# Wider warming matmuls ahead of the memory keys, and three more behind the first six products

## The chip, the cores and the metric

The kernel runs on one core of a Trainium2 chip. The metric is the device time of one execution in microseconds (us), median of several runs; lower is better.

## The reference

One layer of a hybrid decoder trunk in float32: a prompt of 1024 tokens and 8 sample tokens share the weights. Cut to what matters here:

```python
z = x @ w_in                                  # one projection, split among the branches and gates
mkv = (mem_prompt @ w_mem_kv).reshape(1, 256, 2, 4, 256)
mk, mv = mkv[:, :, 0], mkv[:, :, 1]           # memory keys and values, for 256 memory tokens
a_out = rg_lru(causal_conv(xr)) * gelu(yr)
s_out = sliding_window_attention(q, k, v, sinks)
c_out = mem_attn(xq, mk, mv)                  # cross-attention into the memory
merged = sum(gates[n] * (br @ w_branch[n]) for n, br in enumerate((a_out, s_out, c_out)))
h = layer_norm(ALPHA * x + merged @ w_out)
y = layer_norm(ALPHA * h + (silu(h @ w_gate) * (h @ w_up)) @ w_down)
```

`mk` and `mv` are also outputs. `mem_prompt` has 256 rows of 1024, `w_mem_kv` 1024 x 2048.

## The kernel before

The kernel is written with a scheduler that follows the order of the code within the stage at issue (the orders of SP, ACT, DVE and PE are kept as written). Transposed tiles hold features on the 128 partitions and tokens along the free axis. A float32 product is made of three: each operand is cut into a high part (rounded to the multiplier's format, by ACT) and a low part (the rest, by DVE), and `mm3` (lines 128 to 130) issues high x high, high x low and low x high into one PSUM sum. `split` (lines 82 and 83) is that cut: ACT writes the `..h` tile, DVE the `..l` tile.

The program begins with `mem_kv`, which computes the memory keys and values. Its pieces:

- `mem_raw(k)` loads two of the eight feature tiles of the memory, `mem_split(k)` cuts them into `memh`, `meml`; all eight stay as `memx[0]` to `memx[7]`.
- `fetch(n)` loads one half (512 columns) of a weight tile `wm`, n = 0 to 31, five steps ahead; `cut(n)` cuts it into `wm_h` and `wm_l`, three steps ahead. The first half, `wm0`, and the first memory tiles are loaded and cut in two pieces.
- `key(n)` for n = 0 to 15 issues 12 products of 256 columns, four terms of three; two steps make one bank `mk`. `value(n)` for n = 16 to 31 issues 12 products into two banks `mv`. `put` copies a finished bank with ACT and stores it with a DMA from POOL.
- Within the same loop, `x_quarter` loads the input in eight pieces of 516 KB, and `moving` (the generator `combos`) makes sums of them on DVE and cuts them into `th` and `tl` for the projection that follows (`fast_step`, whose products write `ub`, `uc`, `ud`).

The tiles for `wm_h` go round in five buffers and those for `wm_l` in four, so a cut waits until PE has used the tile four or five steps back. The loads go out on SP's queue (two of the first on ACT's), in the order of the code, each into a buffer that a cut has set free.

Ahead of all products stand the warming matmuls (line 503): `WARM` = 20 products of the constant tile `ones` with itself, 128 columns each, into a bank `warm` that nobody reads. They wait only for the memset of `ones`.

Of the kernel before, what the change touches and what calls it, by code (L numbers as in the profile page):

```python
# [18 lines left out]
P = 128  # L19
# [7 lines left out]
NM = 256  # L27
# [6 lines left out]
BANKS = {"mm": 3, "s": 2, "t": 2, "o": 1}  # L34
HT = T // 2
FIRST = 6
WARM = 20
ORDERED = {mybir.EngineType.SP, mybir.EngineType.Activation, mybir.EngineType.DVE, mybir.EngineType.PE}
QN = T // 4
QS = 264  # L40
# [18 lines left out]
class Builder:  # L59
# [380 lines left out]
    def mem_kv(self, moving, xs, load, quarters):  # L440


        nc, io = self.nc, self.io
        h = D // 2
        memx, raws, pairs, sums = [], {}, {}, {}
        order = [(f, p) for f in ((0, 0), (0, 1), (1, 1), (1, 0)) for p in range(2)]

        def put(bank, name, m):
            raw = self.ph.tile([P, 256], F32, tag="kvraw", name=f"{name}r{m}", bufs=4)
            nc.scalar.copy(raw, bank[1][:, :256])  # L450
            self.idle.append(bank[0])
            nc.gpsimd.dma_start(self.scr[name][:, m, :], raw)

        def mem_raw(k, queue=None, pieces=1):
            src = io["memT"][:, 2 * k * NM:(2 * k + 2) * NM]
            raws["mem", k] = self.half_raw(src, 2 * NM, f"mem{k}", k < 3, queue, pieces)

        def mem_split(k, between=()):
            raw = raws.pop(("mem", k))
            for i in range(2):  # L460
                for f in between[:i]:
                    f()
                memx.append(tuple(self.ph.tile([P, NM], F32R, tag="mem", name=f"mem{e}{2 * k + i}", bufs=16)
                                  for e in "hl"))
                self.split(*memx[-1], raw[:, i * NM:(i + 1) * NM])

        def fetch(n, queue=None, pieces=1):
            if n < 16:
                src = io["wmk"][n // 2][:, n % 2 * h:(n % 2 + 1) * h]
            else:  # L470
                src = io["wmv"][(n - 16) // 2][:, n % 2 * h:(n % 2 + 1) * h]
            raws[n] = self.half_raw(src, h, f"wm{n}r", 4 < n < 28 and n % 3 == 0, queue, pieces)

        def cut(n, pieces=1):
            pairs[n] = self.half_pair(f"wm{n}_")
            raw = raws.pop(n)
            for i in range(pieces):
                cols = slice(i * h // pieces, (i + 1) * h // pieces)
                self.split(*(t[:, cols] for t in (*pairs[n], raw)))
                if i + 1 < pieces:  # L480
                    yield

        def key(n):
            m, e = n // 2, n % 2
            if e == 0:
                sums[m] = self.take(f"mk{m}")
            hi, lo = pairs.pop(n)
            cols = [slice(i * P, (i + 1) * P) for i in range(4)]
            self.mm3(sums[m][1][:, :NM], [((hi[:, w], lo[:, w]), memx[4 * e + i]) for i, w in enumerate(cols)], e == 1, e == 0)

        def value(n):
            g, j = (n - 16) // 4, n % 4
            if j == 0:
                sums[g] = [self.take(f"mv{g}_{tt}") for tt in range(2)]
            hi, lo = pairs.pop(n)
            cols = [slice(i * 256, (i + 1) * 256) for i in range(2)]
            for tt in range(2):
                xs_ = [tuple(a[:, tt * P:(tt + 1) * P] for a in memx[2 * j + i]) for i in range(2)]
                self.mm3(sums[g][tt][1][:, :256], [(x, (hi[:, w], lo[:, w])) for x, w in zip(xs_, cols)], j == 3, j == 0)

        warm = self.bank("o", "warm")
        for _ in range(WARM):
            nc.tensor.matmul(warm[:, :P], self.ones, self.ones, start=True, stop=True)
        other = nc.scalar
        for f in (partial(mem_raw, 0, pieces=2), partial(fetch, 0, other, 2), partial(mem_raw, 1, other), partial(fetch, 1),
                  partial(mem_raw, 2), partial(mem_raw, 3), partial(fetch, 2), partial(fetch, 3), partial(fetch, 4)):
            f()
        first, rest = cut(0, 2), lambda n: deque(cut(n), 0)
        mem_split(0, (partial(next, first),))
        deque(first, 0)  # L510
        for f in (partial(mem_split, 1), partial(rest, 1), partial(mem_split, 2), partial(mem_split, 3), partial(rest, 2)):
            f()
        due = -3.5
        for n in range(32):
            if n + 5 < 32:
                fetch(n + 5)
            elif n == 28:
                load()
            if n % 2 == 0 and n < 16:
                (f, th), p = order[n // 2]  # L520
                xs[(f, th), p] = self.x_quarter(f, th, p)
            if n + 3 < 32:
                rest(n + 3)
            elif n > 29:
                quarters[n - 30]()
            due += 0.6
            if due > 0:
                due -= next(moving)
            (key if n < 16 else value)(n)
            if 0 < n <= 16 and n % 2 == 0:  # L530
                put(sums.pop(n // 2 - 1), "mk", n // 2 - 1)
            if n > 16 and n % 4 == 0:
                g = (n - 16) // 4 - 1
                for tt, ps in enumerate(sums.pop(g)):
                    put(ps, "mv", 2 * g + tt)
        for tt, ps in enumerate(sums.pop(3)):
            put(ps, "mv", 6 + tt)
# [1322 lines left out]
```

## Time and profile before

| | |
|---|---|
| time, median of 3 runs | 1896.47 us (1895.70 to 1896.66) |
| span of the profiled execution, first to last instruction | 1894.5 us |
| time around the span, against the median | 1.97 us |
| PE busy (matmuls) | 1880.9 us, 99% of the span |
| DVE / ACT busy | 1398.8 us (74%) / 1056.6 us (56%) |
| DMA | 302.18 MB, 160 GB/s on average |
| waits of PE up to 120 us | 1.1 (start), 0.9 (`memh`), 0.3 (`u2s`) |

The profile gives one execution. A row of the timeline has the start and the duration in us, the engine, the line, the operation, the tiles (buffer numbers left out), the shape, and in square brackets the idle time of that engine ahead of it and what ended it. Matmuls are pipelined: the duration of one holds its way through the array, so the time that it costs is read from start to start. A row of a table by stretches has the stretch, its length, the busy time of PE, PE's weight loads, DVE, ACT and POOL with the number of instructions, then the granted clock of TensorE, the share of the DMA engines in use and GB/s. A value such as 1.04 for that share counts as full.

### The profile page before, as it was taken

What the parts mean: (1) busy time and instruction counts of PE and PEld (TensorE: products, weight loads), DVE (VectorE), ACT (ScalarE), POOL (GpSimd) and SP (SyncE); (2) the same over time, 40 slices, a digit from 0 to 9 for tenths busy, and PEclk for the clock granted to TensorE, in tenths of its full rate; (3) what the DMA queues carried; (4) which work ended last, traced back from release to release, by engine and by line L of the source; (5) the groups of instructions that cost most, each with busy time, mean ns of one, the idle gap of its engine ahead of it and who ended that gap; (6) DMA issues with size and microseconds to landing.
All of it is one profiled execution on the core that took longest, in us unless ns stands there. A gap on an engine that the chain in (4) does not pass through costs nothing.

```text
span 1894.5 us, 38166 instructions
## 1 busy us (share of the span) xinstructions
PE 1880.9 (99%) x14836; PEld 1865.1 (98%) x14836; DVE 1398.8 (74%) x2736; ACT 1056.6 (56%) x2199; POOL 126.7 (7%) x190
## 2 busy tenths in 40 slices
PE   9999999999999999999999999999999999999998
PEld 9999999999999999999999999999999999999998
DVE  7878878888788757579787567776667667858486
ACT  6575676666676656578774234543433433636454
POOL 1000012110000000022210000000000000001200
PEclk9999999999999999999999999999999999999999
DMA  9535345446444377546525251233355235758872
GB/s 333 171 109 171 114 142 172 137 143 221 143 159 152 108 239 253 190 144 198 155 79 188 90 190 57 68 112 115 112 165 199 99 123 185 263 131 271 173 216 90
DMA packets 176261, 302.18 MB, mean 160 GB/s; under 512 B 18944, under 2 KB 93136, under 8 KB 176080
## 3 DMA queue, kind: packets, MB, share of 16 engines
q1 hardware_dynamic: 168976, 280.12, 45.0%
q0 software_dynamic: 4224, 14.78, 4.0%
q10 hardware_dynamic: 2880, 4.85, 0.7%
q8 instruction: 116, 1.90, 0.4%
q14 instruction: 65, 0.53, 0.1%
HBM read 217.97 MB, written 85.89 MB: 160 GB/s over the span
## 4 chain that ended last, share of the span: by engine, by line
PE 92%; DVE 3%; DMA 2%; ACT 1%; issue 1%; SPq 0%; ACTq 0%; DVEq 0%
PE ub L271 5%; PE ub L273 5%; PE ub L272 5%; PE ubfg L272 4%; PE ubfg L273 4%; PE ubfg L271 4%; PE ud L273 3%; PE ud L272 3%; PE ud L271 3%; PE udfg L271 2%; PE udfg L272 2%; PE udfg L273 2%; PE ubf L271 2%; PE op L128 2%; PE ubf L272 2%; PE ubf L273 2%
## 5 line engine op out<-in xcount | busy, mean ns | idle before, releaser
L712 ACT ACTIVATE bp<-bp,bst 128x257 f32<-128x257 f32 (+1 forms) x128 | 62.9, 493 | 37.3 <-DVE bst L706 37.2
L271 PE MATMUL ub<-th,u_6h 128*128 128x258 f32 x240 | 68.8, 287 | 1.9 <-DVE zb L312 1.8
L706 DVE CUSTOM_DVE_ANT_0 bp<-bs,mask,nsnk 128x256 f32<-128x256 f32 (+1 forms) x128 | 55.8, 462 | 19.0 <-PE bs L703 18.6
L271 PE MATMUL ub<-th,u_4h 128*128 128x258 f32 x240 | 68.2, 284 | 0.3 <-ACT u2s L305 0.3
L273 PE MATMUL ud<-th,u_5l 128*128 128x258 f32 x240 | 68.2, 284 | 0.0
L271 PE MATMUL ud<-th,u_5h 128*128 128x258 f32 x240 | 68.1, 284 | 0.0
L271 PE MATMUL ub<-th,u_0h 128*128 128x258 f32 x240 | 68.1, 284 | 0.0
L273 PE MATMUL ud<-th,u_1l 128*128 128x258 f32 x240 | 68.1, 284 | 0.0
L271 PE MATMUL ub<-th,u_2h 128*128 128x258 f32 x240 | 68.1, 284 | 0.0
L273 PE MATMUL ub<-th,u_4l 128*128 128x258 f32 x240 | 68.0, 284 | 0.0
L271 PE MATMUL ud<-th,u_1h 128*128 128x258 f32 x240 | 68.0, 284 | 0.0
L273 PE MATMUL ub<-th,u_2l 128*128 128x258 f32 x240 | 68.0, 284 | 0.0
L273 PE MATMUL uc<-th,u_3l 128*128 128x258 f32 x240 | 68.0, 283 | 0.0
L271 PE MATMUL uc<-th,u_3h 128*128 128x258 f32 x240 | 68.0, 283 | 0.0
L273 PE MATMUL ub<-th,u_0l 128*128 128x258 f32 x240 | 68.0, 283 | 0.0
L273 PE MATMUL ub<-th,u_6l 128*128 128x258 f32 x240 | 68.0, 283 | 0.0
L272 PE MATMUL ud<-tl,u_5h 128*128 128x258 f32 x240 | 67.7, 282 | 0.0
L272 PE MATMUL ub<-tl,u_0h 128*128 128x258 f32 x240 | 67.6, 282 | 0.0
L272 PE MATMUL ub<-tl,u_6h 128*128 128x258 f32 x240 | 67.6, 282 | 0.0
L272 PE MATMUL ub<-tl,u_4h 128*128 128x258 f32 x240 | 67.6, 282 | 0.0
L272 PE MATMUL ud<-tl,u_1h 128*128 128x258 f32 x240 | 67.6, 282 | 0.0
L272 PE MATMUL uc<-tl,u_3h 128*128 128x258 f32 x240 | 67.6, 282 | 0.0
(959 smaller groups left out, 8257.6 us busy)
## 6 DMA issues: line engine op xcount, KB each, us to landing
ur<-win SPq DMA_DIRECT2D x120, 256.0 KB, 3.0
urfg<-wgu SPq DMA_DIRECT2D x80, 256.0 KB, 2.7
scr_f<-G SPq DMA_DIRECT2D x22, 516.0 KB, 2.9
f<-scr_f SPq DMA_DIRECT2D x16, 516.0 KB, 4.0
fs<-scr_t SPq DMA_DIRECT2D x16, 516.0 KB, 7.2
dck<-cmk SPq DMA_DIRECT2D x32, 256.0 KB, 4.4
dcv<-cmvT SPq DMA_DIRECT2D x32, 256.0 KB, 4.6
urf<-wdn SPq DMA_DIRECT2D x32, 256.0 KB, 3.4
```

The lines of the kernel that those rows point to most:

```text
L128: nc.tensor.matmul(ps, sh, mh, start=opens and i == 0, stop=False)
L271: mm(sh[:, w], xh, start=opens and k == 0, stop=False)
L272: mm(sh[:, w], xl, start=False, stop=False)
L273: self.last_mm = mm(sl[:, w], xh, start=False, stop=k == 3).ins
L706: nc.vector.tensor_tensor_reduce(pg[g], s[:, u * 256:u * 256 + n], msk, 1.0, snk[:, g:g + 1], ALU.add, ALU.min, st[:, g:g + 1])
L712: nc.scalar.activation(x, x, AF.Exp, bias=st[:, g:g + 1], scale=-1.0, accum_out=st[:, 4 + g:5 + g])
```

## The change

The warming matmuls are ten instead of twenty, and each has 512 columns instead of 128: the moving operand is now the first column of `ones`, read 512 times. Three more of them stand in `key(0)`, behind its first two terms (six products). The sum of `key(0)` is otherwise the same and is made in the same order.

```diff
-WARM = 20
+WARM = 10
...
-            self.mm3(sums[m][1][:, :NM], [((hi[:, w], lo[:, w]), memx[4 * e + i]) for i, w in enumerate(cols)], e == 1, e == 0)
+            terms = [((hi[:, w], lo[:, w]), memx[4 * e + i]) for i, w in enumerate(cols)]
+            if n == 0:
+                self.mm3(sums[m][1][:, :NM], terms[:2], False, True)
+                keep_warm(3)
+                self.mm3(sums[m][1][:, :NM], terms[2:], False, False)
+            else:
+                self.mm3(sums[m][1][:, :NM], terms, e == 1, e == 0)
...
-        for _ in range(WARM):
-            nc.tensor.matmul(warm[:, :P], self.ones, self.ones, start=True, stop=True)
+
+        def keep_warm(n):
+            for _ in range(n):
+                nc.tensor.matmul(warm, self.ones, self.ones[:, 0:1].to_broadcast([P, 512]), start=True, stop=True)
+
+        keep_warm(WARM)
```

On PE, at the start of the program, stand before (L503 the warmers, L128 to L130 the products of `key(0)`; `memh0` to `memh2` are the high parts of the first three memory tiles, `wm0_h` and `wm0_l` the two parts of the first weights; the number behind the last underscore is a running one):

```order
L503 MATMUL warm_143<-ones_61 128x128 x20
L128 MATMUL mk0_238<-memh0_184,wm0_h_188 128x256
L129 MATMUL mk0_238<-meml0_185,wm0_h_188 128x256
L130 MATMUL mk0_238<-memh0_184,wm0_l_189 128x256
L128 MATMUL mk0_238<-memh1_192,wm0_h_188 128x256
L129 MATMUL mk0_238<-meml1_193,wm0_h_188 128x256
L130 MATMUL mk0_238<-memh1_192,wm0_l_189 128x256
L128 MATMUL mk0_238<-memh2_198,wm0_h_188 128x256
```

and at the same place now, with L511 for the warmers:

```order
L511 MATMUL warm_143<-ones_61 128x512 x10
L128 MATMUL mk0_228<-memh0_174,wm0_h_178 128x256
L129 MATMUL mk0_228<-meml0_175,wm0_h_178 128x256
L130 MATMUL mk0_228<-memh0_174,wm0_l_179 128x256
L128 MATMUL mk0_228<-memh1_182,wm0_h_178 128x256
L129 MATMUL mk0_228<-meml1_183,wm0_h_178 128x256
L130 MATMUL mk0_228<-memh1_182,wm0_l_179 128x256
L511 MATMUL warm_143<-ones_61 128x512 x3
L128 MATMUL mk0_228<-memh2_188,wm0_h_178 128x256
```

Ten wide warmers replace the twenty, and three stand between the product of `memh1` with `wm0_l` and the first product of `memh2`. All other rows of PE, and all rows of ACT, DVE, POOL and SP, keep their order.

## The prediction

> **What bounds the kernel now.** I read the page first (busy time, the chain that ended last), then PE's waits, then the timeline of the first 70 us, engine by engine. The first two lines are from the page, the third from the list of PE's waits up to 120 us.
>
> ```profile
> PE 1880.9 (99%) x14836; PEld 1865.1 (98%) x14836; DVE 1398.8 (74%) x2736; ACT 1056.6 (56%) x2199; POOL 126.7 (7%) x190
> PE 92%; DVE 3%; DMA 2%; ACT 1%; issue 1%; SPq 0%; ACTq 0%; DVEq 0%
> ...
> PE mk L128 <- ACT memh L82: 0.9, 1, 0.9
> ```
>
> PE sets the time, so a microsecond taken from PE early reaches the end only if PE does not wait it away again. The change touches the first 8 us. PE's rows there (start, duration, and in brackets the idle time before):
>
> ```profile
> 1.05 4.53 PE L503 MATMUL warm<-ones 128*128 128x128 f32 x20 [1.05 <-DVE lruc L839]
> 5.38 0.52 PE L128 MATMUL mk<-memh,wm_h 128*128 128x256 f32 x1
> ...
> 6.55 0.41 PE L130 MATMUL mk<-memh,wm_l 128*128 128x256 f32 x1
> 7.88 0.58 PE L128 MATMUL mk<-memh,wm_h 128*128 128x256 f32 x1 [0.91 <-ACT memh L82]
> ...
> 8.94 0.41 PE L128 MATMUL mk<-memh,wm_h 128*128 128x256 f32 x1
> ...
> 9.79 0.57 PE L129 MATMUL mk<-meml,wm_h 128*128 128x256 f32 x1
> 10.15 0.41 PE L130 MATMUL mk<-memh,wm_l 128*128 128x256 f32 x1
> ...
> 12.29 0.41 PE L128 MATMUL mk<-memh,wm_h 128*128 128x256 f32 x1
> ...
> 13.57 0.41 PE L128 MATMUL mk<-memh,wm_h 128*128 128x256 f32 x1
> 13.78 0.33 PE L129 MATMUL mk<-meml,wm_h 128*128 128x256 f32 x1
> 13.95 0.28 PE L130 MATMUL mk<-memh,wm_l 128*128 128x256 f32 x1
> 14.07 0.28 PE L128 MATMUL mk<-memh,wm_h 128*128 128x256 f32 x1
> ```
>
> Starts of equal products lie 0.21 us apart up to 13.78 (13.78 - 13.57) and 0.12 from 13.95 on (14.07 - 13.95). That is a clock that doubles at about 13.85. The granted-clock column does not show it (1.00 in the first of the rows below), but shows a half clock at the end, where PE has stopped (second row):
>
> ```profile
> 13.00:13.80 0.80, 0.80 (x6) 0.80 (x6) 0.28 (x1) 0.62 (x1) 0.57 (x1) 1.00 0.99 389
> 1888.00:1889.00 1.00, 0.00 (x0) 0.00 (x0) 1.00 (x3) 1.00 (x4) 0.00 (x0) 0.50 0.02 7
> ```
>
> So PE starts at half clock, and 4.3 us of 128-column warmers, six products, a pause of 1.1 us and six more microseconds of products pass before it is let go. A warmer takes 4.27/20 = 0.213 us, as long as a product with twice its columns: PE streams half of the time. What opened the clock were dense 256-column products: without a pause from 8.94 (4.9 us) but for one bubble (9.79 to 10.15), or 4.1 us counted from 9.79.
>
> **The change, part by part.** *The first warmers.* At half clock 512 columns take 2 x 0.213 = 0.427 us, ten take 4.27, so they end at 1.05 + 4.27 = 5.32 as the twenty did. At full clock 512 columns take 0.235 (761.70 - 761.47 here, in a later stage):
>
> ```profile
> 761.47 0.40 PE L136 MATMUL co<-cph,mv 128*128 128x512 f32 x1
> 761.70 0.40 PE L137 MATMUL co<-cph,mv 128*128 128x512 f32 x1
> ```
>
> If the clock opens among them they end earlier, which gains nothing: the sixth product needs the second half of wm0_l, ready at 5.73 (first row), and behind it all wait for the second piece of the memory, whose cast comes at 7.43 (second row), when it has landed. Term: 0.
>
> ```profile
> 5.31 0.42 DVE L83 TENSOR_TENSOR wm_l<-wm0r,wm_h 128x256 fp32r<-128x256 f32 x1
> ```
> ```profile
> 7.43 0.71 ACT L82 CAST memh<-mem 128x256 fp32r<-128x256 f32 x2 [2.18 <-DMA mem<-memT]
> ```
>
> *The three warmers in the pause.* They start when the sixth product has streamed, at 6.55 + 0.21 = 6.76, and take 3 x 0.427 = 1.28 at half clock (to 8.04, 0.16 past the 7.88 of the seventh product) or 3 x 0.235 = 0.70 at full (to 7.5). Bounds 0 to +0.16; I take 0, as the clock should be open by then. What covers them is the 0.91 us wait; nothing but products queues behind them.
>
> *The clock.* PE now streams densely from 1.05. With 4.1 to 4.9 us of it needed, as above, the clock opens between 5.2 and 6.0, ahead of the pause. From 7.88 to 13.95 PE issues 26 products in 6.07 us; at 0.118 they need 3.07. Bound of the gain: -3.0. The data allow less:
>
> ```profile
> 9.30 1.43 DVE L83 TENSOR_TENSOR meml<-mem,memh 128x256 fp32r<-128x256 f32 x4
> 10.64 0.69 DVE L83 TENSOR_TENSOR wm_l<-wm2r,wm_h 128x512 fp32r<-128x512 f32 x1
> ```
>
> The last term of key(1) needs the fourth of these meml, ready at 10.73, so key(1) ends at about 11.0 instead of 12.29. key(2)'s third product needs wm2_l at 11.33; ten products from there end at 12.54. Before, the product of 14.07 is key(2)'s tenth, and the key ends at 14.43. PE is then 14.43 - 12.54 = 1.9 us ahead. Term: -1.9.
>
> *Who waits for what next.* From 14.43 on a key or value step is 12 x 0.118 = 1.414 us. Its cut (wm_h on ACT, then wm_l on DVE) was far ahead of PE at key(3), but comes closer, since it runs at the pace of the loads (ACT and DVE rows; then two stretches, with the DMA's share and GB/s last):
>
> ```profile
> 23.77 0.62 ACT L82 CAST wm_h<-wm12r 128x512 fp32r<-128x512 f32 x1 [1.67 <-DMA wm12r<-wmk]
> ...
> 29.57 0.62 ACT L82 CAST wm_h<-wm16r 128x512 fp32r<-128x512 f32 x1 [1.01 <-DMA wm16r<-wmv]
> ```
> ```profile
> 24.43 0.69 DVE L83 TENSOR_TENSOR wm_l<-wm12r,wm_h 128x512 fp32r<-128x512 f32 x1 [0.48 <-ACT wm_h L82]
> ...
> 28.00 0.69 DVE L83 TENSOR_TENSOR wm_l<-wm14r,wm_h 128x512 fp32r<-128x512 f32 x1
> ...
> 30.22 0.69 DVE L83 TENSOR_TENSOR wm_l<-wm16r,wm_h 128x512 fp32r<-128x512 f32 x1 [0.94 <-PE mk L130]
> ...
> 31.49 1.23 DVE L216 TENSOR_TENSOR x<-x,x 128x1032 f32<-128x1032 f32 x1
> ...
> 35.05 0.68 DVE L83 TENSOR_TENSOR wm_l<-wm18r,wm_h 128x512 fp32r<-128x512 f32 x1
> ```
> ```profile
> 8.00:30.00 22.00, 22.00 (x162) 21.75 (x163) 17.42 (x26) 15.32 (x30) 3.42 (x6) 1.00 1.04 399
> ...
> 13.00:15.00 2.00, 2.00 (x15) 2.00 (x15) 0.59 (x2) 1.11 (x2) 0.70 (x1) 1.00 0.94 359
> ```
>
> ACT waits for wm12r and for wm16r to land, while the DMA engines are full (1.04 over 22 us). The row at 30.22 names PE, but key(12), whose tile it reuses, ended at 14.43 + 10 x 1.414 = 28.57; wm16_h ended at 29.57 + 0.62 = 30.19, the same 0.03 to 0.04 ahead as wm12_h (24.39 for 24.43). So the load of wm16 starts this DVE row, and from there DVE has no pause up to wm18_l (six rows, the first and third and the last shown), ready at 35.73. PE at that place, value(18), the 19th step:
>
> ```profile
> 35.69 0.28 PE L128 MATMUL mv<-wm_h,memh 128*128 128x256 f32 x1
> 35.80 0.36 PE L129 MATMUL mv<-wm_l,memh 128*128 128x256 f32 x1
> 36.01 0.28 PE L130 MATMUL mv<-wm_h,meml 128*128 128x256 f32 x1
> ```
>
> The product with wm_l was held here already: the next follows after 0.21 instead of 0.118, 0.09 us lost. key(14) would start at 14.43 + 11 x 1.414 - 1.9 = 28.1 and its third product at 28.3, but wm14_l is ready only at 28.69: 0.4 given back. value(18)'s second product would come at 35.80 - 1.5 = 34.3 and waits for 35.73, the other 1.5. Behind it PE runs as before. Term: +1.9, all of it, if the loads land as before. What is late next is unchanged, the wait of 0.28 at 67.33:
>
> ```profile
> 67.33 0.39 PE L271 MATMUL ub<-th,u_4h 128*128 128x258 f32 x1 [0.28 <-ACT u2s L305]
> ```
>
> *Stores and loads.* A key that is done 1.9 us sooner is stored sooner by POOL, which puts 1.9/2.83 x 131 KB = 88 KB ahead of the loads: at 399 GB/s +0.2, at most one store, +0.33. Fetches that wait for DVE rows, which wait for PE (below: the stores, SP's waits, DVE's waits), go out up to 1.9 earlier, into a full DMA; if it were not full they would pull the landings forward by as much.
>
> ```profile
> scr_mk<-mkr POOLq DMA_DIRECT2D x8, 128.0 KB, 5.4
> ```
> ```profile
> SPq L103 <- DVE wm_l L83: 14.8, 15, 3.8
> ```
> ```profile
> DVE wm_l L83 <- PE mk L130: 4.2, 5, 1.4
> ```
>
> Bounds -1.9 to +0.33. I take +0.1, nearest to the row with share 1.04.
>
> *Sum* against the profiled execution (span 1894.5, with 1.97 us around it to the median of 1896.47): 0 + 0 - 1.9 + 1.9 + 0.1 = +0.1. One term more is against the median: in an execution whose clock opens after 13.85, PE reaches value(18) later than wm18_l and carries the lateness on, since only 0.09 us of wait covers it. The three runs spread over 0.96 us; an early clock brings all to the fast end (1895.70). Half the spread, -0.5. Forecast: 1896.47 + 0.1 - 0.5, rounded to 1896.1, no change by the 0.2% (3.8 us) that a measurement of this kernel can tell.
>
> [...]
>
> **The rivals.** *Kept gain.* The loads of wm12 to wm18 land earlier, because their issues do; PE keeps 0.5 to 3.0 us: 1893.5 to 1896.0, with -1.9 at 1894.6. For it: the DMA share of 0.94 at 13 to 15 us. Against it: 1.04 over the whole.
>
> *The repeated column.* The new moving operand is one column of ones read 512 times; no row here has one. With r times the time for a column, the first warmers end at 1.05 + 4.27r, and with six products (0.7), three warmers (0.705r) and 42 products (4.96), key(3) ends at 6.7 + 4.98r instead of 15.85. With r = 4 that is 26.6, 10.8 late, less the waits of 0.09 and 0.28: 1906.9, slower. It decides from r = 2.7 (20.1, 3.8 late after the waits). Against it: all moving operands here stream at the same columns per time (0.118 for 256, 0.235 for 512).
>
> [...]
>
> *The clock closes again* in the new waits of 0.4 and 1.5 us, and PE needs some 4.1 us at 0.213, 4.1 x 0.45 = 1.8 late: 1898.0. Against it: after the wait below the durations were 0.28 again, the full clock's.
>
> ```profile
> 579.49 0.39 PE L271 MATMUL ub<-th,u_6h 128*128 128x258 f32 x1 [1.34 <-DVE zb L312]
> ```
>
> **How the numbers follow.** Forecast (gain made and given back) 0.66; kept gain 0.18; clock not earlier 0.06; clock closes again or loads land later 0.06; repeated column 0.04. The range 1894.4 to 1897.2 holds the forecast, the third case and two thirds of the kept gain, and leaves out some 0.16. Faster by over 0.2% needs more than the bound of 3.0 us, 0.02; slower is the repeated column, 0.04; the rest, 0.94, is no change.
>
> **What would show it.** Right: PE's products 0.118 apart from 7.88 on; key(2) done near 12.5; a new PE wait of about 1.5 us at 34 to 36 us for DVE wm_l, and a smaller one near 28; the rows from 36.01 on at their old times within 0.3. Wrong: wm16_h cast well before 29.5 (kept gain), products at 0.21 after 8 (the clock did not open), warmers that end after 5.4 (the column).

## The result, and the profile after

The changed kernel takes 1898.96 us (median of 21 runs, 1896.68 to 1902.38), the kernel before 1896.34 in the same sessions (21 runs, 1894.33 to 1898.36): ratio 1.0013, interval 1.0008 to 1.0019. The change costs 2.6 us. That is inside the 3.8 us that the prediction called no change, but outside its range (1894.4 to 1897.2), and it has the other sign. The profiled execution took 1898.75 us, span 1897.0, 2.5 more than before.

The page, PE's busy time with the number of matmuls, and the queue that loads code (packets, MB, share):

```profile
PE 1880.9 (99%) x14829; PEld 1863.5 (98%) x14829; DVE 1398.6 (74%) x2736; ACT 1056.1 (56%) x2199; POOL 125.9 (7%) x190
...
q8 instruction: 116, 1.90, 0.4%
```

Busy time is the same to 0.1 us, with seven matmuls fewer. The opening did what was forecast (timeline of PE):

```profile
1.05 4.64 PE L511 MATMUL warm<-ones 128*128 128x512 f32 x10 [1.05 <-DVE lruc L849]
5.48 0.42 PE L128 MATMUL mk<-memh,wm_h 128*128 128x256 f32 x1
...
6.34 0.38 PE L129 MATMUL mk<-meml,wm_h 128*128 128x256 f32 x1
6.55 0.28 PE L130 MATMUL mk<-memh,wm_l 128*128 128x256 f32 x1
6.67 0.82 PE L511 MATMUL warm<-ones 128*128 128x512 f32 x3
7.33 0.28 PE L128 MATMUL mk<-memh,wm_h 128*128 128x256 f32 x1
...
11.81 0.28 PE L130 MATMUL mk<-memh,wm_l 128*128 128x256 f32 x1
11.93 0.28 PE L128 MATMUL mk<-memh,wm_h 128*128 128x256 f32 x1
```

The clock opens at about 6.5, where the duration falls from 0.42 to 0.28 and the distance to 0.12; before, that was at 13.9. The last row is the first product of `key(3)`, so key(2) is done at 11.93, 2.5 us sooner than before. Some of it is not the change's: the second memory piece came 0.74 us sooner here (its cast at 6.69 instead of 7.43), as it did, at 6.7 to 7.0, in most later executions of either kernel. At `value(18)` part of the lead is given back; the rows are DVE's, then PE's:

```profile
33.75 0.68 DVE L83 TENSOR_TENSOR wm_l<-wm18r,wm_h 128x512 fp32r<-128x512 f32 x1
```
```profile
34.49 0.39 PE L129 MATMUL mv<-wm_l,memh 128*128 128x256 f32 x1 [1.02 <-DVE wm_l L83]
34.71 0.28 PE L130 MATMUL mv<-wm_h,meml 128*128 128x256 f32 x1
```

The product at 34.71 was at 36.01 before: PE goes on with a lead of 1.3 us. Laying PE's rows of both traces side by side, the distance (after less before) is -1.2 at 49, -0.9 at 179, -1.1 at 365 and still -1.1 at 514. Then it turns: +0.1 at 579.5, +1.6 at 582, +2.4 at 864, +2.5 at the end. Against this profile of before the loss lies behind 514 us, most of it within 3 us around 580, a place that the change does not touch. There stands a wait that was 1.34 us before (the row that the prediction quoted at 579.49). Timeline of PE after:

```profile
579.59 0.39 PE L271 MATMUL ub<-th,u_6h 128*128 128x258 f32 x1 [2.57 <-DVE zb L312]
579.82 0.28 PE L272 MATMUL ub<-tl,u_6h 128*128 128x258 f32 x1
579.93 0.37 PE L273 MATMUL ub<-th,u_6l 128*128 128x258 f32 x1
580.10 0.42 PE L271 MATMUL ub<-th,u_6h 128*128 128x258 f32 x1
580.32 0.42 PE L272 MATMUL ub<-tl,u_6h 128*128 128x258 f32 x1
```

Two things are seen: the wait for `zb` is 2.57 us, and behind it the clock halves (0.42 us, 0.215 from start to start). The table by stretches shows it in the granted clock, third number from the end, and again full at 583.4; the first fence is after, the second before:

```profile
580.00:582.00 2.00, 2.00 (x11) 2.00 (x11) 2.00 (x4) 0.69 (x1) 0.00 (x0) 0.50 0.00 0
582.00:583.40 1.40, 1.40 (x9) 1.40 (x8) 1.40 (x4) 1.40 (x4) 0.00 (x0) 0.50 0.00 0
583.40:585.00 1.60, 1.60 (x15) 1.60 (x15) 1.60 (x2) 1.60 (x4) 0.00 (x0) 1.00 0.13 54
```
```profile
580.00:582.00 2.00, 2.00 (x19) 2.00 (x19) 2.00 (x4) 0.79 (x1) 0.00 (x0) 1.00 0.00 0
```

Eleven products in 2 us instead of nineteen. What PE waits for stands on DVE. Its rows, before and then after:

```profile
578.66 0.43 DVE L976 SCALAR_TENSOR_TENSOR dcj<-dcv,dcvq 128x256 f32<-128x256 f32 x1 [2.99 <-DMA dcv<-cmvT]
579.01 0.08 DVE L976 DVE_READ_ACCUMULATOR dcj<-dcv,dcvq 128x1 f32 x1
579.01 0.42 DVE L312 SCALAR_TENSOR_TENSOR zb<-ub,p5s 128x258 f32<-128x258 f32 x1
```
```profile
578.76 0.42 DVE L986 SCALAR_TENSOR_TENSOR dcj<-dcv,dcvq 128x256 f32<-128x256 f32 x1 [4.22 <-DMA dcv<-cmvT]
579.11 0.08 DVE L986 DVE_READ_ACCUMULATOR dcj<-dcv,dcvq 128x1 f32 x1
579.11 0.42 DVE L312 SCALAR_TENSOR_TENSOR zb<-ub,p5s 128x258 f32<-128x258 f32 x1
```

`dots` (L976, after L986) makes the row sums of the sample tokens' attention into the memory. It waits for a load (`dcv`, 256 KB); `zb`, whose operands are there, stands behind it on DVE, and PE waits for `zb`. By the semaphores of the trace this is the last `dcv` load but one, issued at 572.89 before and 571.77 after; the last one landed at 579.19 and 579.31, behind the row sum. The load was issued 1.1 us sooner after, as all was; yet its row sum starts 0.1 later. From issue to row sum it took 5.77 us before and 6.99 after. The trace has 16 landings for this load, one for each part of it. After, 15 of them had landed by 577.33 and the last came 1.31 us behind, at 578.64; before, the last two came 0.41 apart. So one part of sixteen was late. Why is what the experiments ask.

### The profile page after: what moved, and what is told of

The parts are those of the page before. It is cut to its first block, busy times and chain, and to the rows that moved or that the text cites. A ratio compares the mean times of both kernels' runs of the same rounds, so it can differ in the third digit from the quotient of the medians.

```text
span 1897.0 us, 38152 instructions
## 1 busy us (share of the span) xinstructions
PE 1880.9 (99%) x14829; PEld 1863.5 (98%) x14829; DVE 1398.6 (74%) x2736; ACT 1056.1 (56%) x2199; POOL 125.9 (7%) x190
## 4 chain that ended last, share of the span: by engine, by line
PE 91%; DVE 4%; DMA 3%; issue 1%; ACT 1%; SPq 0%; ACTq 0%; DVEq 0%
PE ub L271 5%; PE ub L273 5%; PE ub L272 5%; PE ubfg L272 4%; PE ubfg L271 4%; PE ubfg L273 4%; PE ud L273 3%; PE ud L272 2%; PE ud L271 2%; PE udfg L271 2%; PE udfg L272 2%; PE udfg L273 2%; PE ubf L271 2%; PE op L128 2%; PE ubf L272 2%; PE ubf L273 2%
```

## The experiments

The expectations name theory G: PE's lead of 1.2 us, won at the start, moves PE against the loads near 579. Its rival, I, came to be: the number of PE instructions ahead matters, because PE's code is itself loaded by DMA (taken to be the 116 packets of `q8 instruction`), and that load moves against the `dcv` loads. Times are medians; in brackets stands the kernel before in the same session.

### The two kernels again

No edit.

> The kernel before, profiled a second time. Theory G (an early PE waits longer at 579 us for the row sums behind the dcv loads, and a pause of about 2 us or more there closes TensorE's clock for one stretch of 3.4 us, about 1.5 us lost): PE's wait near 579 is 1.0 to 1.7 us, the clock stays 1.00 from its opening (12 to 15.5 us) to the end, median 1896.0 to 1896.8. Rival I (the changed number of instructions shifts the code and the loads, the clock has no part in it): the same time, but the wait near 579 and the clock are as they may be, not tied to where PE stands at 550 us.

> The changed kernel, profiled a second time. Theory G: the clock opens between 4.4 and 8 us, PE runs 0.8 to 2 us ahead of the kernel before from 36 to 570 us, waits 2 to 3.2 us near 579, and the granted clock shows 0.50 for 3.4 us behind that wait; median 1898 to 1900. Rival I: the median too, but no closing of the clock, and the loss in small pieces behind 600 us.

Before: 1896.60 (1897.10). After: 1899.17 (1897.10), ratio 1.0018, 1.0009 to 1.0028. The loss repeats. Two of the 12 executions of after took 1905.7 and 1906.2 us; what happened in them is not known. In this execution of before the clock opened at 8.97 instead of 13.9, sooner than expected, and it had the lead over the first profile of before that the changed kernel had: at 36 us PE stands 1.17 us ahead, 0.1 behind the changed kernel's. It lost nothing at 579:

```profile
576.67 0.43 DVE L976 SCALAR_TENSOR_TENSOR dcj<-dcv,dcvq 128x256 f32<-128x256 f32 x1 [3.02 <-DMA dcv<-cmvT]
```

Issue (570.87) to row sum is 5.80 us, as before. That speaks against G already: the same lead, not the same loss. It did not keep the lead either. Small waits took it further on, and its span is 1895.2, 0.7 over the first one's (two rows of PE):

```profile
739.29 0.50 PE L139 MATMUL co<-cpl,mv 128*128 128x512 f32 x1 [0.42 <-DVE cpl L83]
...
863.94 0.50 PE L740 MATMUL bo<-bph,vs 128*128 128x512 f32 x1 [0.83 <-ACT bph L82]
```

The second execution of after (issue to row sum 6.03, wait 1.6 us) kept its full clock at 579 and ended 0.8 behind the second one of before. Against that one it lost 0.6 us near 178 and 0.25 at 579: so the place at 579, which cost most in the first profile, is not the only one.

### PE held back again (five wide warmers behind the values)

```diff
                     put(ps, "mv", 2 * g + tt)
+        keep_warm(DELAY)                      # DELAY = 5, near 54 us
```

> The changed kernel, with five more warming matmuls of 512 columns (1.18 us of PE time at full clock) behind the last product of the memory values, at about 51 us. They compute nothing that is used. Theory G: PE then stands about where it stood before the change, the wait near 579 is 1.0 to 1.7 us, the clock stays open, and the kernel is FASTER than the changed one by 1.5 to 3 us: 1896 to 1897.5. Rival I: PE does 1.2 us more, nothing is given back: 1899 to 1901.

1897.25 (1897.10), ratio 1.0003, 0.9994 to 1.0011; the wait at 579 is 0.7, in an execution of 1894.71, the fastest of the eleven. The loss is gone, as G expected. But five more matmuls also bring the count from 7 too few to 2 too few, so that this run tells G from I no more.

### The sample loads one step earlier, with and without the change

```diff
-            t = ph.tile([P, 512], F32, tag="dk", name=f"dc{kind}{b}_{h}", bufs=3)
+            t = ph.tile([P, 512], F32, tag="dk", name=f"dc{kind}{b}_{h}", bufs=4)
...
         fetch("k", 1)
+        fetch("k", 2)
...
-                fetch("k", b + 2)
+            if b + 3 < NB:
+                fetch("k", b + 3)
             else:
-                fetch("v", b + 2 - NB)
+                fetch("v", b + 3 - NB)
...
-                fetch("v", b + 2)
+            if b + 3 < NB:
+                fetch("v", b + 3)
```

> The changed kernel, with the loads of the sample group's memory rows (dck, dcv) one step earlier and one more buffer for them (four, not three). Theory G: DVE's wait for dcv near 575 to 579 goes, and with it PE's wait at 579 (under 0.5 us) and the closing of the clock; the early PE's 1.1 us are kept to 600 us and the 1.34 us wait of the kernel before is gained as well: 1894 to 1896.5. Rival I: the loads were not the cause of the loss, 1897.5 to 1899.

> The kernel before, with the loads of the sample group's memory rows (dck, dcv) one step earlier and a fourth buffer, as in the run of the changed kernel with earlier loads (1895.27). Theory G: the wait near 579 (1.3 to 1.4 us in two profiles of before) goes under 0.5 us, and the kernel gains about that: 1894.8 to 1896.2. With that wait gone, the change itself is worth 0 to -1 us: this run ends 0 to 1 us behind 1895.27. Rival I (the change loses by shifted code, whatever the loads do): this run is faster than 1895.27 by 1.5 us or more.

With the change: 1895.27 (1897.10), ratio 0.9993, 0.9984 to 1.0001; PE does not wait at 579 at all. So the sample loads are what PE waited for, and the loss goes with the wait. Without the change: 1893.31 (1896.09), ratio 0.9987, 0.9978 to 0.9995. There PE's wait stayed at 0.8 us where under 0.5 was expected (list from 560 to 600 us): the row sum no longer waits for `dcv`, which had landed 10 us earlier, but for the rows `dcvq`, whose load stands where it stood.

```profile
PE ub L271 <- DVE zb L312: 0.8, 1, 0.8
```

Each against its own session, this kernel is 2.8 below before and the other 1.8; G expected the changed kernel in front or level, I expected this one in front by 1.5 us or more, as it came (2.0). The intervals overlap, so this speaks against G only weakly. In the profiled executions the changed kernel is 0.8 behind up to 577 us, level from 580 to 740, and loses 0.8 there and 0.8 near 860, in waits such as this (list of PE's waits from 600 to 1000 us, with the change; 0.3 without it):

```profile
PE bo L750 <- ACT bph L82: 1.0, 1, 1.0
```

### Work put into the wait, only to hold the clock

```diff
+            if (u, i, p) == FILL and self.idle is not None:      # FILL = (24, 6, 1)
+                fill = self.bank("o", "fill")
+                for _ in range(6):
+                    nc.tensor.matmul(fill, self.ones, self.ones[:, 0:1].to_broadcast([P, 512]), start=True, stop=True)
             self.fast_product(st, i, p, ts, ps, i in (0, 1, 3))
```

> The changed kernel, with six 512-column matmuls that compute nothing used (1.41 us at full clock) put into PE's queue at the place of its wait near 579 us, ahead of the product that waits. Theory G: PE is busy through most of the wait, the clock never closes there, mean granted clock 0.998 in nearly all executions, and the median falls from about 1899 to 1897.2 to 1898.2; the wait left over is 0 to 1.2 us. Rival I: the clock's closing is not what costs, and 1.4 us more of matmuls bring nothing or a loss: 1898.8 to 1900.5.

1897.62 (1896.09), ratio 1.0008, 1.0000 to 1.0017: 1.5 us over before instead of 2.6 and 2.1 without the filling. PE's rows there:

```profile
578.30 1.47 PE L305 MATMUL fill<-ones 128*128 128x512 f32 x6
579.63 0.39 PE L272 MATMUL ub<-th,u_6h 128*128 128x258 f32 x1
579.85 0.28 PE L273 MATMUL ub<-tl,u_6h 128*128 128x258 f32 x1
579.97 0.28 PE L274 MATMUL ub<-th,u_6l 128*128 128x258 f32 x1
```

The clock holds, and by the medians 0.6 to 1.1 us of the loss are gone, but the intervals with and without the filling overlap, so this is not shown. Nor does this execution test a long wait: the row sum started 5.58 us after the issue, as quickly as before, and the wait to be filled was 1.3 us. And the six matmuls bring the count of PE instructions from 7 too few to 1 too few for all that follows, so that what is gained behind 579 need not be the clock's.

### The two parts of the change apart

```diff
-                keep_warm(3)
+                keep_warm(0)          # the wide warmers only
```
```diff
-        keep_warm(WARM)
+        for _ in range(WARM):         # WARM = 20: the narrow warmers of before, and the three wide ones
+            nc.tensor.matmul(warm[:, :P], self.ones, self.ones, start=True, stop=True)
```

> The changed kernel without the three warmers behind the first six products: the ten of 512 columns alone. Theory G: ten wide ones are enough to open the clock before 8 us, so this is the changed kernel again: 1898 to 1900, PE ahead by 0.8 to 2 us from 36 to 570 us, and a wait near 579 of 1.6 us or more. Rival I, or if the three are what opens the clock: it opens later than 8.5 us and the time is that of before, 1896 to 1897.5.

> The twenty warmers of 128 columns of the kernel before, and the three of 512 columns behind the first six products. Theory G: PE streams densely from 5.4 us on, the clock opens between 7 and 12.3 us; PE is back on the loads' pace at 36 us in any case, and so the time is between before and changed, 1896.5 to 1899. If the clock opens as early as 8 us here too, the loss is that of the changed kernel (1898 to 1900) without any of the wide ones ahead.

Wide only: 1899.31 (1896.09), ratio 1.0017, 1.0008 to 1.0026. Three only: 1896.23 (1896.09), ratio 1.0000, 0.9991 to 1.0008, though its clock opened at 8.4 and PE had the same lead at 36 us as the changed kernel, within 0.1. Wide only had no lead at 36 us (0.1), against what G expected, and lost; three only had the lead and did not. The loss comes with the first part, which takes ten matmuls away, and not with the lead.

Wide only also shows what the three are for. The clock opened at 5.9 and closed at 9.35, behind a pause that they fill in the change (PE's rows, and a stretch of the table):

```profile
8.76 0.38 PE L128 MATMUL mk<-memh,wm_h 128*128 128x256 f32 x1 [2.20 <-ACT memh L82]
...
9.72 0.41 PE L128 MATMUL mk<-memh,wm_h 128*128 128x256 f32 x1
9.93 0.41 PE L129 MATMUL mk<-meml,wm_h 128*128 128x256 f32 x1
...
12.74 0.30 PE L129 MATMUL mk<-meml,wm_h 128*128 128x256 f32 x1
12.88 0.28 PE L130 MATMUL mk<-memh,wm_l 128*128 128x256 f32 x1
```
```profile
9.40:12.70 3.30, 3.30 (x15) 3.13 (x16) 3.23 (x8) 3.30 (x9) 0.00 (x0) 0.50 1.02 370
```

### The count of PE instructions, at equal warmth

The queue `q8 instruction` on the page has 116 packets with 1.90 MB, 16 KB each; that they are PE's code is the author's reading, and what speaks for it is that they move with the number of PE's instructions (table below). PE has 14836 + 14836 instructions, matmuls and weight loads, in before; divided by 116 that is an estimate of 256 for each packet, or 128 products, some 15 us of work, and the packets start 15.6 us apart in the median. With seven fewer ahead, each packet should then come when PE is 7 x 0.12 = 0.84 us further in the program. The trace shows a median of 0.82 over all packets. Where the packet near 573 us stands is bracketed by the tables of DMA for a window, of before from 573 to 574 us (the two `dcv` issues are in it too), and of after from 575 to 576, behind the issues of 571.8 to 572.9:

```profile
q8 instruction: 1, 0.02, 7.0%
issues: line engine op xcount, KB each, median us to landing
dcv<-cmvT SPq DMA_DIRECT2D x2, 256.0 KB
```
```profile
q1 hardware_dynamic: 277, 0.30, 97.2%
q8 instruction: 1, 0.02, 5.8%
```

7.0% of the time of 16 engines in 1 us is 1.1 us of one engine; 5.8% are 0.9 us. The packet itself took 1.1 and 0.9 us. Before it was fetched while the loads were being issued, after in the midst of their transfer. This packet moved by more than the median: by 3.3 us of PE's program, and by 2.5 to 4.1 in all kernels below with seven or ten matmuls fewer, the filled one (1.4) aside. Why it moved so far is open. Moved by 0.8 us alone it would already come just behind the issues of the loads, and no longer ahead of the last one. Three kernels change the count: the change with 17 first warmers of 300 columns (20 matmuls in all, as before), before with 13 narrow warmers (7 fewer, nothing wide), and the change with 20 of 256 columns (23 in all). A fourth has 20 in all and the earlier loads.

```diff
-WARM = 10
+WARM = 17                             # (20 with 256 columns)
...
-        keep_warm(WARM)
+        keep_warm(WARM, 300)          # columns (or 256)
```
```diff
-WARM = 20
+WARM = 13                             # in the kernel before
```

> The changed kernel with seventeen warmers of 300 columns ahead instead of ten of 512 (the same 5100 columns and the same time), and the same three behind the first six products: twenty warmers in all, as many PE instructions as before. Theory I (now refined: the 16 KB loads of PE's code come every 128 products; seven products fewer ahead put each of them 0.82 us later in the program, and near 575 us among the dcv loads, whose landing they hold up; the longer wait then closes the clock): the code load near 573 falls back beside the issue of dcv (within 0.5 us of it), the wait near 579 is 1.0 to 1.7 us, no closing there, median 1895.5 to 1897, 2 to 3 us faster than the changed kernel. Theory G (PE's lead alone makes the wait): as the changed kernel, 1898 to 1900.

> The kernel before with thirteen warmers of 128 columns instead of twenty, nothing else: as many PE instructions as the changed kernel, none of them wide. Theory I: it loses like the changed kernel, the code load near 575 comes 2.5 to 4 us behind the issue of dcv, wait near 579 of 1.6 us or more, 1898 to 1900. Theory G: the clock opens at 9 to 15 us as before and the time is that of before, 1896 to 1897.2.

> The changed kernel with twenty warmers of 256 columns ahead instead of ten of 512, the same columns, and the three behind: 23 warmers, three PE products more than before, as in the run with the twenty narrow ones and the three. Theory I: the code loads come 0.3 us earlier in the program than before, and the time is that of that run, 1895.5 to 1897. Theory G: as the changed kernel, 1898 to 1900.

> Seventeen warmers of 300 columns, the three behind the first six products, and the dck and dcv loads one step earlier: the early clock, the old instruction count and no wait near 579. Theory I: as the kernel before with earlier loads (1893.3) or up to 1 us faster, 1892 to 1893.8. Theory G: 1894.5 to 1896, as the changed kernel with earlier loads (1895.3).

Same count: 1895.45 (1895.80), ratio 1.0003, 0.9994 to 1.0012: wide warmers, three in the pause, clock open at 5.8, and no loss. Thirteen narrow: 1899.40 (1895.80), ratio 1.0020, 1.0010 to 1.0029: none of the change but seven matmuls fewer, and all of the loss in the median (3.6 us). Its profiled execution is the fastest of the eleven, 1897.55, and lost 0.7 at 579. PE's wait at 579 in these two (lists from 560 to 600 us; total, times, longest):

```profile
PE ub L271 <- DVE zb L312: 1.2, 1, 1.2
```
```profile
PE ub L271 <- DVE zb L312: 2.0, 1, 2.0
```

Count 23: 1895.52 (1895.80), ratio 1.0001, 0.9992 to 1.0009. Same count with the earlier loads: 1893.74 (1895.80), ratio 0.9990, 0.9981 to 0.9999, not to be told from 1893.31 of the kernel before with the same loads. Both beat the two kernels, the second of them with a wait of 1.2 us left at 577, for the `dcvq` rows; what the warmers add to it can't be measured.

### The seven given back later

```diff
                     put(ps, "mv", 2 * g + tt)
+        for _ in range(7):            # near 54 us, in before with 13 warmers, and in the change
+            nc.tensor.matmul(warm[:, :P], self.ones, self.ones, start=True, stop=True)
```

> The kernel before with thirteen narrow warmers ahead (1899.4 alone) and seven more narrow matmuls, used by nothing, behind the last product of the memory values at about 52 us (some 0.5 us of PE time). Theory I: from there on the 16 KB code loads of PE come at the same products as before, the code load near 573 beside the issue of dcv, and the time is that of before: 1895.5 to 1897.2. Rival O (the loss is made in the opening, by fewer warmers): 1899 to 1900.5, with the 0.5 us on top.

> The changed kernel, ten wide warmers and three, with the same seven narrow matmuls at 52 us. Theory I: 1895.3 to 1897.2, and no closing of the clock near 579 us. Rival O: 1898.5 to 1900.

The change with seven: 1896.17 (1895.78), ratio 1.0003, 0.9994 to 1.0012; the wait is 0.6 and the loss gone. Seven idle matmuls, which take PE's own time (0.7 us from the first to the row behind them), bring it back. Before with 13 and seven: 1897.63 (1895.78), ratio 1.0011, 1.0002 to 1.0020: half the loss is gone (3.6 to 1.9) and the packet is back in its place with a wait of 1.4, but half stays. The seven themselves cost 0.7. The other 1 us is about as large as a wait of 0.86 us at 95.67 in the profiled execution, for `zb` behind the row sums of an earlier load, which before does not have. The change with seven has one of 1.60 there and is level all the same, so that this stays open.

All of them side by side. "Count" is PE's matmuls ahead of 570 us against before, "moved" how much later in PE's program the code packets come (median of the packets, at PE's pace of before; of the filled kernel those ahead of its filling), "packet" the start of the packet near 573 us less the last `dcv` issue, "landing" the time from the issue of the `dcv` load that the row sum waits for to that row sum, "last part" how far the last of this load's 16 parts landed behind the next to last. These are read off the profiled executions. The last column has the medians of all runs; a profiled execution need not be a typical one, and the columns ahead of it do not add up to it.

| kernel | count | moved, us | packet | landing | last part | wait at 579 | time less before |
|---|---|---|---|---|---|---|---|
| before; again | 0 | 0; 0.0 | -0.2; -0.1 | 5.77; 5.80 | 0.4; 0.4 | 1.3; 1.4 | 0; -0.5 |
| three only | +3 | -0.32 | -0.1 | 5.86 | 0.1 | 1.4 | +0.1 |
| count 23 | +3 | -0.30 | -0.1 | 5.22 | 0.1 | 0.8 | -0.3 |
| same count | 0 | 0.01 | -0.2 | 5.61 | 0.6 | 1.2 | -0.4 |
| change and seven late | 0 | -0.01 | -0.1 | 5.00 | 0.0 | 0.6 | +0.4 |
| 13 and seven late | 0 | -0.02 | 0.0 | 5.79 | 0.1 | 1.4 | +1.9 |
| five wide late | -2 | 0.20 | 0.0 | 5.17 | 0.0 | 0.7 | +0.2 |
| filled wait | -7 | 0.75 | +1.2 | 5.58 | 0.1 | (filled) | +1.5 |
| change; again | -7 | 0.82; 0.83 | +3.1; +2.7 | 6.99; 6.03 | 1.3; 0.6 | 2.6; 1.6 | +2.6; +2.1 |
| 13 narrow | -7 | 0.78 | +2.3 | 6.44 | 0.9 | 2.0 | +3.6 |
| wide only | -10 | 1.26 | +3.9 | 7.29 | 1.8 | 2.9 | +3.2 |

Where the packet comes with the issues or 1.2 us behind them, the row sum starts within 5.86 us; where it comes 2.3 to 3.9 behind them, it takes 6.0 to 7.3. The last `dcv` load ahead of the row sums near 178 us shows the same. In seven of these executions (both of the change, the filled wait, 13 narrow, wide only, the first profile of before, 13 and seven late) a packet starts 2.7 to 4.4 us behind its issue, and its last part lands 1.4 to 1.9 us behind the next to last. Where the packet starts at most 1.9 us behind it, the last part is at most 0.8 late. The load ahead of it, nearer its end when the packet came, has no such part (at most 0.7). The change, 13 narrow and wide only lost 0.6 to 0.9 us there against before again.

That the count decides is shown: 20 and 13 narrow warmers, and 20 and 13 matmuls with the wide ones, without and with the loss, at the same early clock in the second pair. That the packet itself, on one of the DMA engines that also carry the load, is what holds up one part of it, is the reading that fits the late part, but is not shown by itself: no run moved the packet and kept all else, and the trace does not tell which engine carried what.

How the 2.6 us divide is known roughly: the places near 178 and 579 and the closing of the clock differ from execution to execution. Of the 21 runs of the change, the 7 whose mean granted clock reads 0.998 average 1897.4, 1.1 over before; the other 14, at 0.997 or less, 1899.7. A stretch of 3.413 us at half clock, as the change's, lowers that mean by an estimated 3.413/2/1897 = 0.0009, so the sign is as coarse as its last digit, and with 13 narrow warmers the 7 of 11 executions at 0.998 were 3.4 slower than before all the same.

## Why the prediction was wrong

- *First warmers, 0; three warmers, 0.* Right. The ten ended by 5.5 and the three filled the pause, from 6.67 to 7.33, at full clock (0.22 us each, no more than the 0.235 of 512 ordinary columns at 761.47 in before).
- *The clock, 5.2 to 6.0, worth 1.9 us.* Nearly right: 6.5 in the profiled execution, and 4.0 to 6.5 in all the runs with wide warmers; key(2) was done 2.5 us sooner. It opened 3.0 to 5.5 us after the first warmer; what spreads it so is not shown. In none of these runs was it as late as in before (8.97 to 13.9); the prediction gave 0.06 to a clock that opens no earlier. The trace of the change has it open at 6.545 and closed from 579.984 to 583.397, for 3.413 us; the two ends of that stretch lie 168.0 and 169.0 times 3.413 us behind the opening.
- *All of it given back at wm14_l and wm18_l.* Half right. The wait for wm18_l was there, 1.02 instead of 1.5, none near 28, and 1.3 us of lead stayed, since wm16 came 1.3 sooner (its cast at 28.23 instead of 29.57). That is the size of the kept-gain rival up to 514 us, where PE was 1.1 ahead, but not its cause: wm16 came as soon in before again (28.38) and in 13 and seven late (28.14), whose clocks opened at 8.97 and 11.8. The first profile of before, on which the sum was built, was a late one. No kernel with the change as it stands kept the lead to the end.
- *Stores and loads +0.1, early clock -0.5.* Not seen. Three only, count 23 and same count have the early clock, and end at +0.1, -0.3 and -0.4, which their runs can't tell from nothing.
- *The step that failed:* "Behind it PE runs as before." The sum stopped at 36 us. It costed the warmers by their time and left out that there are seven fewer, which moves the code loads through the rest of the program (0.82 us in the median); a term of +2.6 was missing, and none of the rivals has it. That the time came out within the 0.2% called no change is luck: the term that was left out happens to be smaller than that. The wait that it hit, 1.34 us at 579.49, was quoted in the prediction, but as evidence on the clock and not as the place with no slack.
- *The clock closes again (0.06, 1898.0).* It did close, but elsewhere, and my argument against it proved too little. It closed behind a 2.57 us wait in the change and a 2.20 us one in wide only, not behind one of 1.34, and not behind one of 2.86 near 579 in wide only: the length of the wait alone did not decide. The price was some 1.5 us (11 products in 2 us instead of 19, for 3.4 us) against 1.8 in the text.

## What to carry to other kernels

Taking seven to ten instructions from a long unrolled program moved the later loads of its code by 0.78 to 1.26 us in the median; where the bound engine has a place with no slack behind a DMA, a cost of 2 to 4 us turned up, hundreds of us away. Before a small gain or loss is put down to the edit, run the edit's instruction count without its purpose (here 13 narrow warmers) and its purpose at the old count. And mend the place itself: one more buffer and a load one step earlier gave 1.8 to 2.8 us in three kernels, more than the warmers could, though it took the wait at 579 away in only one of them and left 0.8 and 1.2 us in the others.

## What the runs showed of the hardware

- The 116 packets of `q8 instruction`, 16 KB each and by the estimate above 256 instructions of PE, took 0.9 us or more each (1.0 in the median), among the data loads. Their place in the program moved by 0.82 us for 7 matmuls fewer, 1.26 for 10 and -0.32 for 3 more, in the median; a single one by up to 4.1.
- Two pauses were followed by a half clock, and a longer one was not. In wide only, PE idled for 2.20 of the 3.41 us from 5.94 to 9.35 and the clock closed for exactly the next 3.41; in the change, for 2.57 of the 3.41 us from 576.57 to 579.98, where it closed for 3.41. In wide only the longest wait, 2.86 us near 579, left the clock open; why is not shown. The next products start 0.12 apart, at 580.92 and 581.04, the full clock's distance (PE's row behind the wait):

```profile
580.70 0.39 PE L271 MATMUL ub<-th,u_6h 128*128 128x258 f32 x1 [2.86 <-DVE zb L312]
```

- Waits of 1.34, 1.62 and 2.0 us near 579 left the clock open in the profiled executions of before, of after again and of 13 narrow warmers.
- After narrow warmers the clock opened later: behind twenty of 128 columns, 4.27 us, at 9.0 to 13.9 in the kernel before; behind ten of 512 columns in the same time at 4.0 to 6.5. In the first profile of before 4.3 us of narrow warmers and 1.4 us of products, in a row from 1.05 us on, left the clock shut; in the filled kernel it opened at 4.01, after 3.0 us of wide ones.
